# First layer's recurrence: the state-free part made for eight chunks at once, a short chain left

## The chip, the core and the metric

The kernel runs on one core of one Trainium2 chip. Its engines work from queues of their own: PE multiplies matrices into PSUM, DVE and POOL work on vectors, ACT evaluates functions and copies, SP and POOL issue the transfers. The metric is the device time of one execution in microseconds, lower is better; between runs it varies by some tenths of a per cent.

## What is computed

Two layers of a streaming encoder, 2048 tokens of width 1024, all in float32. The change is in the first layer: a state of 64x64 for each of 12 heads, updated token by token.

```python
def step(state, inp):
    r_t, w_t, k_t, v_t, kk_t, a_t = inp
    sa = jnp.einsum('bhvk,bhk->bhv', state, -kk_t)
    state = (state * w_t[:, :, None, :]
             + sa[..., None] * (kk_t * a_t)[:, :, None, :]
             + v_t[..., None] * k_t[:, :, None, :])
    y_t = jnp.einsum('bhvk,bhk->bhv', state, r_t)
    return state, y_t
...
for l in range(DEPTH):
    h = rms_norm(x, pre_norm[l])
    # l = 0: proj = h @ a_w_in, y_br = rwkv7_time_mix(z, ...)
    # l = 1: y_br = diff_attention(q, k_sh, v_sh, ...)
    y_mem = memory_cross_attention(q_mem, mem_n, w_mem_kv[l])
    y = concatenate([y_br * silu(gate), y_mem * silu(g_mem)]) @ w_out[l]
    x = x + rms_norm(y, post_norm[l])
```

`kk_t` is the key times a gain, normalised to length one in each head (`rsqrt` of the sum of its squares); `a_t` is a sigmoid and `w_t` the decay, both from small projections.

## The kernel before

The first layer works in 24 steps: 2 halves of the sequence, in each 6 pairs of heads, in each 2 blocks of 512 tokens. A block has 8 chunks of 64 tokens. Within a chunk the recurrence is solved as a triangular system of 64x64, so that only the state passes from chunk to chunk. A step is an object with these parts (line numbers are those of the kernel before):

- `p1`: the projections of key, receptance and value for 512 tokens (`pj`, L174: 24 products of 128x512 each, hi and lo parts of weights and input in turn), the small products `lr` (L323, L324), decay and sigmoid (`cum`, `asg`), the key's normalisation `pss`/`rn` (L341 to L348), and the operands `AR` and `BK` of the chunk products.
- `p2`: products `pg` of all chunks (L380), masked to `Gm` on DVE (L383); transposes `BKT` (L391) and `UV`.
- `p3`: the triangular inverse `TT`. On DVE a chain of 15 dependent pairs of small operations (`itmp` L431, `Ti` L433), set into two transposed copies (`T16` L440, `TT16` L444); then on PE the products `inv` (L455, twice), `invz` (L468) and `invr` (L474).
- `p4`: the chain over 8 chunks. Each: `xy` (L493, L496), a copy `xs` on ACT, `us` (L502), a copy `UV` on DVE (L503), `sps` (L507), the new state `sb` on DVE (L510), with the decayed state `SP` made on POOL (L491), and the output `xy` (L513).
- `p5`: the norm of the output over each head, a transpose `py` (L535), gate, store.

The loop at the end of `layer_a` traces `p4(i)`, `p5(i)`, `p2(i+1)`, `p3(i+1)` and then `filler(i+2)`: the gate projection of step i+1 (again 24 `pj`) and `p1` of step i+2. From that the framework's scheduler makes, when the program is built, a fixed order for each engine; each engine then works through its order and waits at its head. PSUM tiles come from rings: `pj`, `lr`, `pbn` share three banks under the tag `pj`; most others use two under `gm`, the chain three of its own.

Of the kernel before, what the change touches and what calls it, by code (L numbers as in the profile page):

```python
# [59 lines left out]
def hybrid_kernel(ctx, tc, S, HALF, x, mem, pv, cv, dist, postn, w_out, w_mkv, a_w, w2, a2, w_kv, b_w, out):  # L60
# [68 lines left out]
    def rstd_(xt, junk, ss):  # L129
        """junk: where the squares go; ss: a column for each part of the rows"""  # L130
# [5 lines left out]
    def rows_T(xt, ps, dst, eng):  # L136
        """512 columns of 128 rows, transposed, to each hi, lo of dst, with its gain; eng rounds to hi"""
# [13 lines left out]
    def norm_T(rows, dst, pool, W, PS, xt=None, ptag="gm", eng=nc.sync, junk=None):  # L151
        """128 rows of DRAM (or xt), normalised and transposed into each hi, lo of dst, with its gain"""
# [26 lines left out]
    def mem_T(h, m0, W, PS, pool):  # L179
        """the memory, normalised for both layers, transposed"""  # L180
# [4 lines left out]
    def mem_kv(h, tile_, W, load, PS):  # L185
        """for both layers, keys (hi over lo) and values of the memory, to DRAM"""
# [22 lines left out]
    def layer_a(ph):  # L209
# [46 lines left out]
        def PS(shape, name, tag="gm", bufs=2):  # L256
# [49 lines left out]
        class Step:  # L306
            """one head pair, one block of TB tokens"""
# [4 lines left out]
            def p1(self):  # L312
# [23 lines left out]
                kk2 = W([P, TB], "kk2")  # L336
                A.activation(kk2, kk, AF.Square)
                pss = PS([P, NJ, 2], "pss")
                for c in range(NC):
                    rows = slice(64, 128) if c % 2 == 0 else slice(0, 64)  # L340
                    mm(pss[rows, c // 2, :], lhsT=kk2[:, c * C:(c + 1) * C], rhs=bsum, start=True, stop=True)  # L341
                rn = T([P, NC, 2], "rn", 3)
# [307 lines left out]
        for i in range(n):  # L650
# [626 lines left out]
```

## Time and profile before

| | |
|---|---|
| runs of the program, median (lowest to highest of 3) | 3232.57 us (3231.21 to 3237.78) |
| span of the profiled execution, first to last instruction | 3242.7 us, 10.1 us (0.3%) above that median |
| busy share: PE, DVE, ACT, POOL | 95%, 62%, 44%, 29% |
| mean granted TensorE clock | 0.977 |
| chain that ended last | PE 76%, DVE 14%, ACT 4% |

The span is what the trace counts; no other time is given for the profiled execution itself. Busy shares are means over the whole span; the 24 steps take the stretch from about 70 to 1560 us, the second layer the rest. A busy PE is not a PE at its peak, since starts of matmuls overlap; where a price matters, it is read from the time between starts.

### The profile page before, as it was taken

The page shows a single profiled execution, that of the slowest core. Times are in us where ns is not written, and L with a number is a line of the kernel's source. Part 1 is how long each engine was busy: PE and PEld are TensorE (multiplying, and loading weights), DVE is VectorE, ACT ScalarE, POOL GpSimd, SP SyncE. Part 2 cuts the span into 40 slices and gives each one's busy share as a digit, 9 for nine tenths or more (in the row PEclk, how much of TensorE's full clock was granted, in tenths as well). Part 3 has the DMA queues.
Part 4 walks back from the last instruction along what each step waited for, and adds up shares of the span by engine and source line. Part 5 has one row for each costly group of instructions (what it writes and reads, how often), then busy time and mean ns, then how long its engine had stood idle before and what let it go on. Part 6 is the DMA issues. An engine that isn't in the chain of part 4 may idle for free.

```text
span 3242.7 us, 53751 instructions
## 1 busy us (share of the span) xinstructions
PE 3074.5 (95%) x20026; PEld 2404.1 (74%) x20026; DVE 2008.1 (62%) x5546; ACT 1421.3 (44%) x3126; POOL 928.4 (29%) x1092
## 2 busy tenths in 40 slices
PE   6899999998899999999899999999999999999999
PEld 4766767676667676767577798898887878877777
DVE  6678777866687878786456411111106888887554
ACT  6524333434443434333345522222315777777443
POOL 3224434443244334433100121312411332222100
PEclk9989999998899999999899999999999999999999
DMA  4201000113210001002554443423436555444453
GB/s 131 75 16 35 27 22 22 34 40 90 57 35 27 23 22 33 29 18 69 136 147 135 134 113 90 117 74 96 117 110 159 118 116 112 102 85 119 118 154 113
DMA packets 266150, 265.21 MB, mean 82 GB/s; under 512 B 16832, under 2 KB 206656, under 8 KB 265760
## 3 DMA queue, kind: packets, MB, share of 16 engines
q1 hardware_dynamic: 237760, 195.31, 20.7%
q0 software_dynamic: 28128, 66.46, 10.1%
q8 instruction: 157, 2.57, 0.3%
q14 instruction: 105, 0.86, 0.1%
HBM read 180.45 MB, written 81.26 MB: 81 GB/s over the span
## 4 chain that ended last, share of the span: by engine, by line
PE 76%; DVE 14%; ACT 4%; issue 3%; DMA 2%; POOL 1%; SPq 0%; DVEq 0%; ACTq 0%; POOLq 0%
PE pj L174 30%; PE po L820 10%; PE o L1135 5%; PE vps L996 4%; PE pg L380 3%; PE s L1094 3%; PE s L1095 2%; PE us L502 2%; PE xy L496 2%; PE tr L1125 2%; PE sps L507 1%; PE xy L493 1%; PE mo L759 1%; PE xy L513 1%; DVE E L1097 1%
## 5 line engine op out<-in xcount | busy, mean ns | idle before, releaser
L174 PE MATMUL pj<-hhi,wh 128*128 128x512 f32 x928 | 395.3, 426 | 2.2 <-DVE hlo L149 1.7
L174 PE MATMUL pj<-hhi,wl 128*128 128x512 f32 x928 | 393.2, 424 | 0.4 <-POOL wl L123 0.4
L174 PE MATMUL pj<-hlo,wh 128*128 128x512 f32 x928 | 385.0, 415 | 0.0
L123 POOL TENSOR_TENSOR wl<-wraw,wh 128x512 fp32r<-128x512 f32 x168 | 221.0, 1327 | 399.8 <-ACT wh L122 372.2
L1097 DVE CUSTOM_DVE_ANT_0 E<-s,dist 128x512 f32<-128x512 f32 (+1 forms) x480 | 276.2, 605 | 35.0 <-PE s L1095 28.9
L174 PE MATMUL pj<-bh,wh 128*128 128x512 f32 x672 | 262.6, 391 | 0.0
L174 PE MATMUL pj<-bl,wh 128*128 128x512 f32 x672 | 262.4, 391 | 0.0
L174 PE MATMUL pj<-bh,wl 128*128 128x512 f32 x672 | 262.3, 390 | 0.0
L1102 ACT ACTIVATE E<-E,nm 128x1920 f32<-128x1920 f32 (+7 forms) x192 | 229.4, 1199 | 59.1 <-DVE nm L1100 58.6
L491 POOL TENSOR_SCALAR SP<-sb,PC 128x128 f32<-128x128 f32 x192 | 119.5, 624 | 469.7 <-DVE sb L510 469.7
L1135 PE MATMUL o<-th,vs 128*128 128x256 f32 (+1 forms) x864 | 211.0, 376 | 2.3 <-ACT th L1128 0.9
L174 PEld LDWEIGHTS pj<-hhi,wh 128*128 128x128 f32 x928 | 178.5, 192 | 45.6 <-ACT hhi L148 3.3
L1094 PE MATMUL s<-ks,qd 128*128 128x512 f32 (+1 forms) x480 | 205.7, 432 | 2.2 <-DVE mx L1097 1.2
L174 PEld LDWEIGHTS pj<-hhi,wl 128*128 128x128 f32 x928 | 177.6, 191 | 38.9 <-POOL wl L123 0.8
L174 PEld LDWEIGHTS pj<-hlo,wh 128*128 128x128 f32 x928 | 178.2, 192 | 33.9 <-issue 0.2
L122 ACT ACTIVATE wh<-wraw 128x512 fp32r<-128x512 f32 x168 | 105.4, 628 | 198.0 <-PE pj L174 138.9
L1135 PEld LDWEIGHTS o<-th,vs 128*128 128x128 f32 x864 | 153.8, 189 | 38.7 <-ACT th L1128 19.4
L514 ACT ACTIVATE ys<-xy 64x128 f32<-64x128 f32 x192 | 52.0, 271 | 297.0 <-PE xy L513 251.5
L1095 PE MATMUL s<-ks,qd 128*128 128x512 f32 (+1 forms) x480 | 176.2, 373 | 0.0
L510 DVE SCALAR_TENSOR_TENSOR sb<-sps,PC,SP 64x64 f32<-64x64 f32 x384 | 108.4, 282 | 64.9 <-PE sps L507 57.0
L174 PEld LDWEIGHTS pj<-bh,wh 128*128 128x128 f32 x672 | 126.6, 188 | 26.4 <-DVE ot L831 0.3
L174 PEld LDWEIGHTS pj<-bl,wh 128*128 128x128 f32 x672 | 126.6, 188 | 26.2
(401 smaller groups left out, 7342.3 us busy)
## 6 DMA issues: line engine op xcount, KB each, us to landing
wraw<-in_a_w SPq DMA_DIRECT2D x126, 256.0 KB, 2.9
qd<-qd_d POOLq DMA_DIRECT2D x48, 512.0 KB, 6.9
mq<-mq POOLq DMA_DIRECT2D x64, 256.0 KB, 4.3
ks<-ks_d POOLq DMA_DIRECT2D x24, 512.0 KB, 6.5
yr<-y_dram SPq DMA_DIRECT2D x31, 384.0 KB, 4.9
xt<-in_x SPq DMA_DIRECT2D x16, 512.0 KB, 5.3
x_dram<-ot SPq DMA_DIRECT2D x16, 512.0 KB, 4.4
wraw<-in_b_w SPq DMA_DIRECT2D x32, 256.0 KB, 3.0
```

What stands on the lines that cost most here:

```text
L122: A.activation(hi[:, ks], raw, AF.Copy)
L123: eng.tensor_tensor(out=lo[:, ks], in0=raw, in1=hi[:, ks].bitcast(F32), op=ALU.subtract)
L174: mm(ps, lhsT=w[a_][:, k, wcol], rhs=h[b_][:, k, tsl], start=n == 0, stop=n == 3 * KT - 1)
L491: G_.tensor_scalar(out=SP, in0=SB, scalar1=PC[:, c:c + 1], scalar2=None, op0=ALU.mult)
L510: V.scalar_tensor_tensor(out=SB[hc, hc], in0=sp[hc, :], scalar=PC[hc, c:c + 1], in1=SP[hc, hc], op0=ALU.mult, op1=ALU.add)
L820: mm(po[hf], lhsT=a_[:, k, :], rhs=b_[hf][:, k, :], start=k == i == 0, stop=k == KT - 1 and i == 2)
L996: mm(ps[:, t, :], lhsT=hT[b][a_][:, k, tsl], rhs=w[b_][:, k, :], start=n == 0, stop=n == 3 * KT - 1)
L1094: mm(ps[:, f:f + w_], lhsT=qd[:, 0, c, qs], rhs=k_[:, c, 0:w_], start=True, stop=False)
L1095: mm(ps[:, f:f + w_], lhsT=qd[:, 1, c, qs], rhs=k_[:, c, 0:w_], start=False, stop=True)
L1097: V.tensor_tensor_reduce(out=e[:, kb * 512:kb * 512 + w], in0=ps[:, 0:w], in1=dt_[:, u0:u0 + w], scale=-SLOPES[h], scalar=3.0e38, op0=ALU. ...
L1102: A.activation(E[c][:, 0:nk], E[c][:, 0:nk], AF.Exp, bias=nm[:, c:c + 1], scale=-1.0, accum_out=nm[:, 2 + c:3 + c])
L1135: mm(po[:, oc], lhsT=vs[kt // 4][:, kt % 4, :], rhs=th[:, rc], start=n == 0, stop=n >= nmm - 2, skip_group_check=True)
```

## The change

`p4` is split. The new `p4` (traced after `p3`, one step ahead) makes for all eight chunks at once what needs no state: transposes `atp`, products `nvp`, both solved with `TT` in `txp`, then for each chunk a 128x128 matrix `MT` (identity plus a product, `mrp`) and a 128x64 matrix `RT`, and it starts the sums `ch` with the chunk's own input. `p4b` is the chain: for each chunk one product with `MT` (128x128 by 128x64) onto `ch`, and one scaled copy on ACT, which is the next state; the outputs `yp` are products with `Gm` and with `RT`. The state is kept as 128x64. The key's normalisation is put into `kk` itself: `pss` is now one product of 128x512 with the block of ones, in the ring `pj`, and its inverse comes from Ln and Exp on ACT and a product on POOL; so `Gm` is a masked copy of 512 columns at once (4 operations instead of 32) and `BKT` a plain copy, now on ACT. `pg` takes the two heads in turn. The second `lr` product uses all 128 rows. The rings: `gm` has three banks, the chain two. Comments went, and two constants of the second layer (`ones`, `epsd`) moved to a pool opened later.

```diff
-pps = str_.enter_context(pool_(name="pps", bufs=2, space=PSUM, side="right"))
+pps = str_.enter_context(pool_(name="pps", bufs=3, space=PSUM, side="right"))
...
-def PS(shape, name, tag="gm", bufs=2):
+def PS(shape, name, tag="gm", bufs=3):
...
-            mm(pl, lhsT=lora[rows, 2], rhs=th[i][rows], start=False, stop=True)
+            mm(pl, lhsT=lora[:, 2 + i], rhs=th[i], start=False, stop=True)
...
-        kk2 = W([P, TB], "kk2")
...
-     
+        rn = W([P, TB], "rn")
+        A.activation(rn, kk, AF.Square)
+        pss = PS([P, TB], "pss", "pj")
+        mm(pss, lhsT=bones, rhs=rn, start=True, stop=True)
+        V.tensor_scalar(out=rn, in0=pss, scalar1=1e-12, scalar2=None, op0=ALU.max)
+        A.activation(rn, rn, AF.Ln)
+        A.activation(rn, rn, AF.Exp, scale=-1.0)
+        G_.tensor_tensor(out=rn, in0=rn, in1=asg, op=ALU.mult)
...
-        G_.tensor_tensor(out=kk, in0=kk, in1=asg, op=ALU.mult)
+        G_.tensor_tensor(out=kk, in0=kk, in1=rn, op=ALU.mult)
...
-        for g in range(2):
+        for e in range(2):
+            pgs = [PS([P, NJ, P], "pg") for hh in range(2)]
+            for j in range(NJ):
+                for hh in range(2):
+                    hs = slice(hh * 64, hh * 64 + 64)
+                    mm(pgs[hh][:, j, :], lhsT=BK[hs, 2 * j + e, :], rhs=AR[hs, 2 * j + e, :], start=True, stop=True)
             for hh in range(2):
-                pg = PS([P, 4, P], "pg")
...
-        BKT = T([P, NC, P], "BKT", 2)
+                V.tensor_tensor(out=Gm[:, e, :, hh, :], in0=pgs[hh], in1=cc(("maskE", "maskO")[e], 128)[:, None, :].broadcast_to([P, NJ, P]), op=ALU.mult)
+        BKT = T([P, NC, P], "BKT", 1)
         for g in range(2):
             pt = PS([P, 4, 2, 64], "bkp")
             for c in range(4):
                 nc.tensor.transpose(pt[:, c].rearrange("p h k -> p (h k)"), BK[:, g * 4 + c, :], ident)
-            V.tensor_tensor(out=BKT[:, g * 4:g * 4 + 4, :].rearrange("p c (h k) -> p (c h) k", h=2),
-                            in0=pt.rearrange("p c h k -> p (c h) k"),
-                            in1=rn[:, g * 4:g * 4 + 4, :].rearrange("p c h -> p (c h)")[:, :, None].broadcast_to([P, 8, 64]), op=ALU.mult)
+            A.activation(BKT[:, g * 4:g * 4 + 4, :], pt.rearrange("p c h k -> p c (h k)"), AF.Copy)
...
-        AR, Gm, BKT, UV, PC = self.AR, self.Gm, self.BKT, self.UV, self.PC
-        ys = self.ys = T([P, NJ, 2, 64], "ys", 1)
-        SB = sb[self.p]
+        AR, Gm, BKT, UV, TT = self.AR, self.Gm, self.BKT, self.UV, self.TT
+        ar = (slice(64, 128), slice(0, 64))
+        rr = (slice(0, 64), slice(64, 128))
+        hcs = (slice(0, 64), slice(64, 128))
+        X = [I([P, 2, 2, P], "X") for g in range(2)]
+        pt = PS([P, NJ, P], "atp")
+        for j in range(NJ):
+            for e in range(2):
+                mm(pt[ar[e], j, :], lhsT=AR[:, 2 * j + e, ar[e]], rhs=ident, start=True, stop=True)
+        for g in range(2):
+            A.activation(X[g][:, :, :, 0:C], pt.rearrange("p j (h k) -> p j h k", h=2)[:, g * 2:g * 2 + 2], AF.Copy, scale=-1.0)
+        pn = PS([P, NJ, 2, C], "nvp")
+        for j in range(NJ):
+            for hh in range(2):
+                for e in range(2):
+                    c = 2 * j + e
+                    mm(pn[ar[e], j, hh, :], lhsT=Gm[rr[e], e, j, hh, ar[e]], rhs=UV[rr[e], c, hcs[hh]], start=True, stop=True)
+        for g in range(2):
+            A.activation(X[g][:, :, :, C:P], pn[:, g * 2:g * 2 + 2], AF.Copy, scale=-1.0)
+        Wn = I([P, NJ, 2, C], "Wn")
+        UV4 = UV.rearrange("p (j e) (h v) -> p j e h v", e=2, h=2)
+        for g in range(2):
+            js = slice(g * 2, g * 2 + 2)
+            px = PS([P, 2, 2, P], "txp")
+            for j in (g * 2, g * 2 + 1):
+                for hh in range(2):
+                    for e in range(2):
+                        mm(px[ar[e], j % 2, hh, :], lhsT=TT[ar[e], j, hh, :], rhs=X[g][ar[e], j % 2, hh, :], start=True, stop=True)
+            A.activation(Wn[:, js], px[:, :, :, 0:C], AF.Copy)
+            for e in range(2):
+                A.activation(UV4[ar[e], js, e], px[ar[e], :, :, C:P], AF.Copy)
+        MT = T([P, NC, P], "MT", 1)
+        MT4 = MT.rearrange("p (j e) k -> p j e k", e=2)
+        RT = T([P, NC, C], "RT", 1)
+        for hh in range(2):
+            G_.memset(MT[hcs[hh], :, hcs[1 - hh]], 0.0)
+        AR4 = AR.rearrange("p (j e) t -> p j e t", e=2)
+        pmr = [PS([P, NJ, P], "mrp") for e in range(2)]
+        for j in range(NJ):
+            for hh in range(2):
+                for e in range(2):
+                    mm(pmr[e][hcs[hh], j, 0:C], lhsT=Wn[ar[e], j, hh, :], rhs=BKT[ar[e], 2 * j + e, hcs[hh]], start=True, stop=True)
+                    mm(pmr[e][hcs[hh], j, C:P], lhsT=Wn[ar[e], j, hh, :], rhs=Gm[ar[e], e, j, hh, rr[e]], start=True, stop=True)
+        for e in range(2):
+            for hh in range(2):
+                hs = hcs[hh]
+                V.tensor_tensor(out=MT4[hs, :, e, hs], in0=pmr[e][hs, :, 0:C], in1=ident[hs, None, hs].broadcast_to([C, NJ, C]), op=ALU.add)
+            V.tensor_tensor(out=RT.rearrange("p (j e) t -> p j e t", e=2)[:, :, e], in0=pmr[e][:, :, C:P], in1=AR4[:, :, e, rr[e]], op=ALU.add)
+        ch = pps.tile([P, NC, C], F32, name="ch", tag="ch", bufs=2)
         for c in range(NC):
-            j, e = c // 2, c % 2
...
-            mm(xy, lhsT=AR[:, c, :], rhs=SB, start=True, stop=True, skip_group_check=True)
             for hh in range(2):
-                hc = slice(hh * 64, hh * 64 + 64)
...
-            A.activation(ys[rr, j].rearrange("p h v -> p (h v)"), xy[rr], AF.Copy)
+                mm(ch[hcs[hh], c, :], lhsT=BKT[:, c, hcs[hh]], rhs=UV[:, c, hcs[hh]], start=c == 0, stop=False, skip_group_check=True)
+        self.MT, self.RT, self.ch = MT, RT, ch
+    def p4b(self):
+        Gm, UV, PC, ch, MT, RT = self.Gm, self.UV, self.PC, self.ch, self.MT, self.RT
+        hcs = (slice(0, 64), slice(64, 128))
+        b = self.t0 // TB
+        S = T([P, NC, C], "S", 1)
+        st = [sb[self.p][:, b % 2]] + [S[:, c] for c in range(1, NC)] + [sb[self.p][:, 1 - b % 2]]
+        for c in range(NC):
+            mm(ch[:, c, :], lhsT=MT[:, c, :], rhs=st[c], start=False, stop=True, skip_group_check=True)
+            A.activation(st[c + 1], ch[:, c, :], AF.Copy, scale=PC[:, c:c + 1])
+        ys = self.ys = T([P, NJ, 2, C], "ys", 1)
+        py = [PS([P, NJ, C], "yp") for hh in range(2)]
+        for hh in range(2):
+            for j in range(NJ):
+                for e in range(2):
+                    rr = hcs[e]
+                    mm(py[hh][rr, j, :], lhsT=Gm[:, e, j, hh, rr], rhs=UV[:, 2 * j + e, hcs[hh]], start=j == 0, stop=False, skip_group_check=True)
+        for j in range(NJ):
+            for e in range(2):
+                for hh in range(2):
+                    c, rr = 2 * j + e, hcs[e]
+                    mm(py[hh][rr, j, :], lhsT=RT[hcs[hh], c, :], rhs=st[c][hcs[hh]], start=False, stop=True, skip_group_check=True)
+        for hh in range(2):
+            A.activation(ys[:, :, hh], py[hh], AF.Copy)
...
-    steps[i].p4()
+    steps[i].p4b()
...
         steps[i + 1].p2()
         steps[i + 1].p3()
+        steps[i + 1].p4()
```

The order of PE changes around the small products. Before, in a regular step (`lr` of the step after next, then the receptance's `pj`, then `inv` of the next step; numbers behind names are tile numbers):

```order
L323 MATMUL lr<-th_9224,lora 128x512
L324 MATMUL lr<-th_9224,lora 128x512
L323 MATMUL lr<-th_9227,lora 128x512
L324 MATMUL lr<-th_9227,lora 128x512
L174 MATMUL pj<-hhi,wh 128x512
L174 MATMUL pj<-hlo,wh 128x512
L174 MATMUL pj<-hhi,wl 128x512
L174 MATMUL pj<-hhi,wh 128x512
L174 MATMUL pj<-hlo,wh 128x512
L174 MATMUL pj<-hhi,wl 128x512
L455 MATMUL inv<-T_10352,E_10292 64x64 x9
```

After the change, at the same place in another regular step:

```order
L174 MATMUL pj<-hlo,wh 128x512
L174 MATMUL pj<-hhi,wl 128x512
L319 MATMUL lr<-th_8434,lora 128x512
L320 MATMUL lr<-th_8434,lora 128x512
L319 MATMUL lr<-th_8437,lora 128x512
L320 MATMUL lr<-th_8437,lora 128x512
L335 MATMUL pss<-rn,cvt 128x512
L442 MATMUL inv<-T_10741,E_10681 64x64 x16
L174 MATMUL pj<-hhi,wh 128x512
L174 MATMUL pj<-hlo,wh 128x512
L174 MATMUL pj<-hhi,wl 128x512
```

The first of the receptance's `pj` has moved behind `pss` and `inv`; ahead of `pss` stand the last of the key's 24 `pj` (22 of them stand between `pg` with its transposes and `lr`) and the four `lr`. Steps of this kind, called A below, are 8 (steps 3, 5, 7, 9, 15, 17, 19, 21). In 11 others, called B, `inv` stands first, then `pss`, then the second `inv`, with nothing between. In A the copy of the first `inv` stands on ACT behind the Ln and Exp of `rn`, and on DVE `TT` behind both `BK`; in B they stand ahead. In steps 1, 11, 12 and 23 there are 41 to 51 `pj` ahead of `inv`.

On PE, the chain before, one chunk and the start of its neighbour's end:

```order
L493 MATMUL xy<-sb_124,AR 128x128
L496 MATMUL xy<-UV,Gm 64x64 x2
L174 MATMUL pj<-hhi,wh 128x512
L174 MATMUL pj<-hlo,wh 128x512
L502 MATMUL us<-xs,TT 64x64 x2
L174 MATMUL pj<-hhi,wl 128x512
L174 MATMUL pj<-hhi,wh 128x512
L174 MATMUL pj<-hlo,wh 128x512
L507 MATMUL sps<-UV,BKT 64x64 x2
L513 MATMUL xy<-UV,Gm 64x64 x2
```

And after, three chunks of the new chain:

```order
L174 MATMUL pj<-hhi,wh 128x512
L174 MATMUL pj<-hlo,wh 128x512
L537 MATMUL ch<-S,MT 128x64
L551 MATMUL yp<-S,RT 64x64 x2
L174 MATMUL pj<-hhi,wl 128x512
L537 MATMUL ch<-S,MT 128x64
L551 MATMUL yp<-S,RT 64x64 x2
L174 MATMUL pj<-hhi,wh 128x512
L174 MATMUL pj<-hlo,wh 128x512
L537 MATMUL ch<-S,MT 128x64
L551 MATMUL yp<-S,RT 64x64 x2
```

Between two links of the chain there are now one or two `pj` instead of some eight; the other `pj` stand in a block ahead of the chain (28 in A, 36 in B) and one behind it (19).

On DVE, what stands ahead of `kk`, which ACT squares for `pss`. Before:

```order
L442 TENSOR_SCALAR X_10348<-Ti,cvt 128x16x16 x2
L280 SCALAR_TENSOR_TENSOR kx<-pj,pvt,kx 128x511
L444 STREAM_TRANSPOSE TT_10356<-X_10348 128x16x32
L538 TENSOR_TENSOR ys<-ys,bon 128x512
L281 SCALAR_TENSOR_TENSOR kx<-carry,pvt,kx 128x1
L326 TENSOR_SCALAR cum<-cum 128x8x64
L282 COPY carry<-pj 128x1
L326 TENSOR_SCALAR asg<-asg 128x512
L458 TENSOR_TENSOR TT<-inv,TT_10356 128x512
L461 STREAM_TRANSPOSE Ta<-TT 128x256
L330 SCALAR_TENSOR_TENSOR cum<-cvt,cum 128x520
L335 TENSOR_SCALAR kk<-kx,pvt 128x512
```

After, in the step of kind A whose PE rows stand above:

```order
L418 TENSOR_TENSOR itmp<-Dd,Ti 128x15
L326 SCALAR_TENSOR_TENSOR cum<-cvt,cum 128x520
L420 TENSOR_TENSOR Ti<-Ti,itmp 128x15
L331 TENSOR_SCALAR kk<-kx,pvt 128x512
L425 TENSOR_SCALAR X_10738<-Ti,cvt 128x16x16 x2
L345 TENSOR_TENSOR AR<-kk,Pt 128x4x128
L427 STREAM_TRANSPOSE T_10741<-X_10738 128x16x32
L429 TENSOR_SCALAR X_10737<-Ti,cvt 128x16x16 x2
L353 COPY PC<-Pt 128x8
L431 STREAM_TRANSPOSE TT_10745<-X_10737 128x16x32
```

In both, `kk` (from the step after next) stands behind the `Ti` chain and behind the scan `cum`; what has moved is what PE holds ahead of `pss`. Ahead of the rows shown there stand in the new order, from the four `Gm` on: two transposes of 64x512, one `e_sil`, two `Dd`, the `Ti` chain, and in it `kx` and the minima of `cum` and `asg`. In B the scan, the transposed copy `T` and `kk` come in this order.

## Rows read from the trace of the kernel before

**Rows 1.** The page's head: span, busy time of PE, granted clock by slice

```profile
span 3242.7 us, 53751 instructions
...
PE 3074.5 (95%) x20026; PEld 2404.1 (74%) x20026; DVE 2008.1 (62%) x5546; ACT 1421.3 (44%) x3126; POOL 928.4 (29%) x1092
...
PEclk9989999998899999999899999999999999999999
```

**Rows 2.** Busy time of a regular stretch: PE, PEld, DVE, ACT, POOL, clock, DMA

```profile
980.00:1460.00 480.00, 460.65 (x3792) 333.62 (x3791) 384.77 (x1117) 175.49 (x386) 189.31 (x225) 0.99 0.09 26
```

**Rows 3.** Line L535 from 900 to 1500 us: ns min/median/max, first and last start

```profile
L535 PE MATMUL py<-cvt,ys x40: 272/273/329, 961.1 to 1456.6; 128*128 128x128 f32 x40
```

**Rows 4.** PE in order of time, one chunk of the chain: start, length in us

```profile
1213.77 0.38 PE L493 MATMUL xy<-sb,AR 128*128 128x128 f32 x2
1214.08 0.44 PE L496 MATMUL xy<-UV,Gm 64*64 64x64 f32 x4
1214.45 0.50 PE L174 MATMUL pj<-hhi,wl 128*128 128x512 f32 x1
1214.79 0.40 PE L174 MATMUL pj<-hhi,wh 128*128 128x512 f32 x1
1215.11 0.44 PE L502 MATMUL us<-xs,TT 64*64 64x64 f32 x4
1215.48 0.50 PE L174 MATMUL pj<-hlo,wh 128*128 128x512 f32 x1
1215.82 0.39 PE L174 MATMUL pj<-hhi,wl 128*128 128x512 f32 x1
...
1216.52 0.39 PE L174 MATMUL pj<-hhi,wl 128*128 128x512 f32 x1
1216.83 0.34 PE L507 MATMUL sps<-UV,BKT 128*64 128x64 f32 x4
1217.00 0.40 PE L513 MATMUL xy<-UV,Gm 128*64 128x64 f32 x4
1217.33 0.50 PE L174 MATMUL pj<-hhi,wh 128*128 128x512 f32 x1
```

**Rows 5.** PE in order of time: other small products and what follows them

```profile
1173.21 0.50 PE L323 MATMUL lr<-th,lora 128*128 128x512 f32 x1
1173.64 0.49 PE L324 MATMUL lr<-th,lora 64*128 64x512 f32 x1
...
1179.59 1.15 PE L455 MATMUL inv<-T,E 64*64 64x64 f32 x32
1180.66 0.50 PE L174 MATMUL pj<-hhi,wh 128*128 128x512 f32 x1
...
1204.28 1.16 PE L380 MATMUL pg<-AR,BK 64*128 64x128 f32 x8
1205.37 0.50 PE L174 MATMUL pj<-hlo,wh 128*128 128x512 f32 x1
```

**Rows 6.** DVE by line and form, 980 to 1460 us: count, busy us, mean ns

```profile
L330 DVE TENSOR_TENSOR_SCAN cum<-cvt,cum 128x520 f32<-128x520 f32 x8 | 14.2, 1775 | 0.8 <-ACT cum L328 0.8
...
L438 DVE TENSOR_SCALAR X<-Ti,cvt 128x256 f32<-128x256 f32 x18 | 12.3, 682 | 0.0
L391 DVE TENSOR_TENSOR BKT<-bkp,rn 128x512 f32<-128x512 f32 x18 | 12.0, 686 | 0.2
...
L440 DVE STREAM_TRANSPOSE T<-X 128x512 f32<-128x512 f32 x9 | 9.4, 1042 | 0.0
...
L280 DVE SCALAR_TENSOR_TENSOR kx<-pj,pvt,kx 128x511 f32<-128x511 f32 x9 | 6.7, 750 | 0.3
```

**Rows 7.** DVE in order of time, inside the `Ti` chain

```profile
1217.90 0.18 DVE L431 TENSOR_TENSOR itmp<-Dd,Ti 128x15 f32<-128x15 f32 x1
...
1219.56 0.21 DVE L433 TENSOR_TENSOR Ti<-Ti,itmp 128x48 f32<-128x48 f32 x1
```

**Rows 8.** ACT by line and form, 980 to 1460 us

```profile
L498 ACT ACTIVATE xs<-xy 64x128 f32<-64x128 f32 x71 | 19.3, 272 | 70.4 <-PE xy L496 69.3
...
L337 ACT ACTIVATE kk<-kk 128x512 f32<-128x512 f32 x8 | 4.9, 614 | 0.0
```

**Rows 9.** Stretches around two drops of the granted clock, columns as in rows 2

```profile
1188.00:1192.00 4.00, 4.00 (x51) 3.20 (x52) 3.39 (x9) 0.26 (x1) 1.27 (x1) 0.50 0.00 0
...
1570.00:1574.00 4.00, 0.00 (x0) 0.00 (x0) 4.00 (x4) 2.23 (x5) 3.49 (x4) 0.51 0.42 117
...
1578.00:1582.00 4.00, 0.21 (x1) 0.21 (x2) 1.61 (x3) 1.99 (x3) 1.62 (x3) 0.50 1.10 386
```

More of the change, by code (lines that the diff above doesn't have):

```diff
@@ L230, in layer_a @@
         for p in range(NPAIR):
-            t = pa.tile([P, P], F32, name=f"sb{p}")
-            G_.memset(t, 0.0)
+            t = pa.tile([P, 2, C], F32, name=f"sb{p}")
+            G_.memset(t[:, 0], 0.0)
             sb.append(t)
@@ L335, in p1 @@
                 V.tensor_scalar(out=kk, in0=kx, scalar1=pc("k_k", p), scalar2=None, op0=ALU.mult)
-                kk2 = W([P, TB], "kk2")
[L337 to L342, printed above, removed]
-                G_.memset(rn, 1.0)
-                rt = TL([P, NJ, 2], "rt", 2)
-                V.tensor_scalar(out=rt, in0=pss, scalar1=1e-12, scalar2=None, op0=ALU.max)
-                rn4 = rn.rearrange("p (j e) h -> p j e h", e=2)
-                V.reciprocal(out=rn4[64:128, :, 0, :], in_=rt[64:128])
-                V.reciprocal(out=rn4[0:64, :, 1, :], in_=rt[0:64])
+                rn = W([P, TB], "rn")
[6 more added lines that the diff above has]
+                G_.tensor_tensor(out=rn, in0=rn, in1=asg, op=ALU.mult)
                 AR = T([P, NC, P], "AR", 2)
@@ L573, in load_lora @@
                     nc.sync.dma_start(out=raw[r:r + 64, i], in_=src[:, p * P:(p + 1) * P])
-            l = pw.tile([P, 3, P], F32R, name="lora", tag="lora", bufs=1)
+            l = pw.tile([P, 4, P], F32R, name="lora", tag="lora", bufs=1)
             A.activation(l[:, 0:2], raw, AF.Copy)
-            for i in range(2):
-                rows = slice(i * 64, i * 64 + 64)
-                G_.tensor_tensor(out=l[rows, 2], in0=raw[rows, i], in1=l[rows, i].bitcast(F32), op=ALU.subtract)
+            G_.tensor_tensor(out=l[:, 2:4], in0=raw, in1=l[:, 0:2].bitcast(F32), op=ALU.subtract)
             return l
@@ L640, in load_mem @@
             return w_
-        mem_kv(memT, lambda sh, n_, dt: T(sh, n_, 2, "BKT", dt=dt), lambda sh, n_: T(sh, n_, 2, "sil"), load_mem, PS)
+        mem_kv(memT, lambda sh, n_, dt: T(sh, n_, 4, "iv", dt=dt), lambda sh, n_: T(sh, n_, 2, "sil"), load_mem, PS)
+        steps[0].p4()
         filler(1)
@@ L1174, in hybrid_kernel @@
     op = layer_a(ph.enter_context(pool_(name="ph", bufs=NB)))
+    const2 = ctx.enter_context(pool_(name="const2", bufs=1, side="right"))
+    ones = const2.tile([P, P], F32, name="ones")
+    epsd = const2.tile([P, P], F32, name="epsd")
     layer_b_proj(ph, op)
```

47 lines of the change are left out of this document (5 added, 42 removed).

## The prediction

> **What bounds the kernel now.** I read the page's head first: PE is busy 95% of the span [rows 1]. Since the change is in the first layer alone, I then asked for a regular stretch of its steps, 980 to 1460 us: PE busy 460.65 of 480 us, 96%, at a clock of 0.99; DVE 80%, ACT 37%, POOL 39% [rows 2]. So here PE's own work sets the time, and the chain's round trips are hidden: PE's order holds `pj` products between every two of its links [rows 4]. How long a step takes I read from the ten transposes `py` of that stretch: 961.1 to 1456.6 us is nine steps, 55.06 us each [rows 3]. Of that PE idles 4%, 2.2 us. The question is therefore not how short the chain gets, but what the change does to PE's work and to PE's waits.
>
> **What is removed.** I price small products by the time from their start to the next group's start, since their lengths overlap. One chunk [rows 4]: `xy` 0.31 (1213.77 to 1214.08), its second part 0.37, `us` 0.37, `sps` 0.17, the output 0.33; together 1.55. A `pj` inside a block takes 0.233 ((1216.52 - 1215.82) / 3), but 0.34 right behind such a group and 0.31 or 0.32 right ahead of one; that is some 0.1 at five such places, 0.49. So a chunk costs PE 2.04 us, a step of eight 16.3 us. The trace shows a loss of time at each change between the small products and the full array. The Trainium skill, "TensorEngine Tiling (Array Packing)", Key Properties, has the reason: changing the tiling mode drains the engine. By the 0.1 of rows 4, the new kernel's nine or so changes a step cost 2 us.
>
> **What is added on PE**, a step, in records (each float32 product is two). The trace has the prices: 0.033 for 64x64 products that go round the quarters of the array (1.07 us for 32, 1179.59 to 1180.66 [rows 5]), 0.043 where the two column halves alternate (`sps`, 0.17 for 4), 0.083 to 0.093 in one quarter, 0.136 (`pg`, 1.09 for 8 [rows 5]) to 0.155 (`xy`) for 128 columns. `atp` 16 x 0.07 = 1.1 (bounds 0.7 and 2.2); `nvp` 32 x 0.033 = 1.1 (to 3.0); `txp`, 128 columns but two halves at a time, 32 x 0.06 = 1.9 (1.1 to 4.4); `mrp`, four records in a quarter and then the next, 64 x 0.052 = 3.3 (2.1 to 6.0); `ch` 32 x 0.043 = 1.4 (to 2.7); the chain 16 x 0.08 = 1.3 (0.7 to 2.5); `yp` from `Gm` 32 x 0.043 = 1.4 (to 2.7) and from `RT` 32 x 0.04 = 1.3 (1.1 to 3.0); changes of tiling 2.0 (1.4 to 3.0). Sum 14.8, bounds 11 and 29; I take 14.8, because nearly all of these are issued in the alternating order that `inv` and `sps` have. `pg` goes from 32 x 0.136 = 4.4 to 3.3, since half of it alternates heads now. PE's work falls by 16.3 - 14.8 + 1.1 = 2.6 us a step. `pss` as one product, `lr` on all rows: nothing, between 0 and -0.7.
>
> **What moves, and what waits.** The order of PE is fixed, and that is where I expect the loss. After `pg` PE holds the transposes, 22 `pj`, four `lr`, and then `pss` or `inv`; the receptance's `pj`, which need neither, come behind. Counted from the start of `py`, PE has until then: `py` 0.6, `pg` 3.3, twelve transposes about 1.6, 22 x 0.233 = 5.1, `lr` 4 x 0.43 = 1.7 [rows 5]: 12.3 us. `pss` needs `kk` from DVE and its square from ACT. DVE can start `Gm` some 2.4 us after `py` starts (transposes, ACT's and DVE's 512 columns, about 0.7 each). Then, in its order: four `Gm` at 0.69 (the nearest row, another 128x512 from PSUM [rows 6]), 2.7; two transposes of 1.04, 2.1; `Dd` and `e_sil`, 1.3 (half and full width, estimates below the 0.69); 30 operations of the `Ti` chain at 0.237 ((1219.56 - 1217.90) / 7 [rows 7]), 7.1; `kx` 0.75 and its two columns, 1.1; the two minima, 0.9; the scan 1.78 [rows 6]; `kk` 0.5. That is 17.5; queued operations overlap a little (-1), and the `Ti` chain must wait for POOL's clearing of `Ti`, which stands behind POOL's work on `Gm` (+1 to +2): 18. With ACT's copy ahead and its square, 0.61 [rows 8], and the hand-overs, `pss` can start 2.4 + 18 + 1.4 = 21.8 us after `py`. PE stands still for 21.8 - 12.3 = 9.5 us; I take 10 (bounds 5 and 13). In B `inv` comes first and needs one more transpose (1.04): the same 10. Before, the chain's own products and their `pj` filled that time: `p4` of the step before lay between `pg` and `inv`.
>
> Behind it: in A, the first `inv` is copied by ACT only after Ln and Exp of `rn`, 0.6 each, and `TT` stands on DVE behind two products that POOL feeds: PE waits 0.4 + 1.4 + 2.0. In B 0.6. In both, `py` comes 0.5 us before its norm is ready, since only 19 `pj` (4.4 us) cover it.
>
> The chain: a link needs PE's product, a copy (0.27 on 64x128 [rows 8]) and two hand-overs, about 0.7; PE has 0.75 to 1.0 of work per link. It costs nothing further; without the `pj` it would be 0.
>
> DVE loses the state's and `UV`'s operations, 28 of 32 `Gm`, and gains six adds; POOL loses `SP`. ACT gains some 5 us a step and stays under half. None of these bounds the whole step; DVE bounds the stretch above because its operations there hang on each other.
>
> **The clock.** After a stretch without products the granted clock is at half: 0.51 and 0.50 with PE idle at 1570 to 1582 us, and 0.50 for 1188 to 1192 us, with PE busy all the time, behind its smallest products [rows 9]. Ten idle microseconds in each step should bring this each time; part of the slow work lies in waits. I take 1.5 us a step (0 to 3.5). The Trainium skill, "TensorE: Matmul & The Clock Gate", HAM oscillation, warns of exactly such idle gaps between blocks of products. By that rule each of the 19 stalls would end at half clock and the cost be nearer the 3.5, some 38 us more in all.
>
> **The sum.** A step of kind A: -2.2 (the old idle time, counted anew) - 2.6 + 10 + 3.8 + 0.5 = +9.5; of kind B: -4.8 + 10 + 0.6 + 0.5 = +6.3. Eight A: 76; eleven B: 69; the other five have 41 to 51 `pj` there or a start of their own, about +1 each, 5; the clock 19 x 1.5 = 28. Together +178 on the profile's 3242.7, 3421; the span lies 10 above the median of the runs, so on the median 3232.6 + 178 = **3410 us**. The first 70 us and the second layer stay.
>
> **Rivals.** (1) *Faster*: DVE's stretch hides and PE stays the bound. Then -2.6 x 24 = -62, and with half of the idle time gone -26 more: 3145 to 3170. It decides at DVE's 18 us: below 9 nothing waits. For it: DVE has lost much work. Against: what was lost lies elsewhere; every operation of the stretch has a row or a near one. 9%. (2) The chain's link is longer than thought, 1.1 to 1.4 us instead of PE's 0.9, so that PE waits at each: 0.4 x 8 x 24 = +77, 3487. Before, `us` started 1.03 us after `xy`'s second part [rows 4], with two `pj` between. The change would then not do what it says, make the chain short. 10%. (3) The small products cost nearer the upper bounds, say 19: +100, 3510. 14%. (4) The losses just cancel: stalls of 3 us a step, no change. 3%. My forecast: 64%.
>
> **Numbers.** Faster 0.09, same (within 0.2%, about what runs of this kernel can tell) 0.03, slower 0.88. The forecast's own range is 3330 to 3480: stalls of 7 to 12 us, clock 0 to 3.5. With rivals (2) and part of (3), and stalls of 5 us below, 3280 to 3520 holds 8 in 10.
>
> **What would show it.** PE busy in a regular stretch down to 80 to 85%; waits of some 10 us at `inv` or `pss`, released by DVE's `T` or ACT's `rn`; a step of 61 to 65 us; half clock once a step behind the wait; DVE busy without a break from `Gm` to `kk`. I am wrong if PE stays above 95% and a step is near 50 us, or if the long waits are at `ch`.

## The result, and the profile after

The changed kernel takes 3376.18 us (3373.14 to 3379.96, three runs): 1.0442 times the kernel before, with a 95% interval of 1.0423 to 1.0461, so 143.6 us slower. The forecast was 178 us slower, and the time lies in the range.

The page's head of the kernel after, beside [rows 1]:

```profile
span 3374.4 us, 57447 instructions
...
PE 3006.6 (89%) x22378; PEld 2437.8 (72%) x22378; DVE 1816.6 (54%) x4728; ACT 1515.2 (45%) x3318; POOL 866.6 (26%) x936
...
PEclk8898998988888898998999999999999999999899
```

The span grew by 131.7 us while PE's busy time fell by 68 us, and DVE lost 191.5 us of work; ACT gained 94 us and stays at 45%. No engine got more to do that could explain the time. The clock's row loses tenths in the first half, where the first layer is. The regular stretch of the first layer (columns as in [rows 2]) and the whole layer from its first `py` to its last, in the kernel after:

```profile
980.00:1460.00 480.00, 396.56 (x4104) 315.75 (x4098) 281.64 (x724) 194.55 (x418) 158.39 (x156) 0.90 0.08 25
179.00:1702.00 1523.00, 1253.93 (x12750) 1000.54 (x12749) 873.99 (x2247) 620.85 (x1356) 472.33 (x463) 0.90 0.12 34
```

The whole layer before, cut the same way:

```profile
193.50:1567.40 1373.90, 1302.97 (x10399) 953.00 (x10399) 1045.49 (x2998) 524.87 (x1163) 522.60 (x601) 0.97 0.13 37
```

PE is busy 83% of the regular stretch, where it was 96% [rows 2], and the clock is 0.90 instead of 0.99. The transposes at a step's start, beside [rows 3]:

```profile
L574 PE MATMUL py<-cvt,ys x40: 270/272/273, 1015.1 to 1567.9; 128*128 128x128 f32 x40
```

Nine steps in 552.8 us, 61.4 us a step against 55.06. What PE waited for in the first layer (engine and line that waited, what it waited for: us in total, times, longest):

```profile
PE inv L442 <- POOL wl L123: 77.5, 8, 9.7
PE pss L335 <- ACT rn L333: 74.3, 11, 8.6
PE inv L442 <- DVE T L427: 49.6, 7, 10.4
PE invz L455 <- DVE Ta L448: 18.1, 8, 2.9
...
PE ch L537 <- ACT S L538: 9.5, 10, 2.3
```

Before, the largest wait at `inv` or `pss` was

```profile
PE inv L455 <- DVE T L440: 13.4, 11, 2.9
```

The waits at `inv` and `pss` are now 201.4 us; those at the chain's products `ch` are 9.5. One wait of the first row, PE in order of time:

```profile
1085.57 0.39 PE L319 MATMUL lr<-th,lora 128*128 128x512 f32 x1
1085.79 0.39 PE L320 MATMUL lr<-th,lora 128*128 128x512 f32 x1
1095.87 1.97 PE L442 MATMUL inv<-T,E 64*64 64x64 f32 x32 [9.69 <-POOL wl L123]
1097.77 2.07 PE L335 MATMUL pss<-rn,cvt 128*128 128x512 f32 x2
```

and DVE at the same time:

```profile
1093.55 1.22 DVE L326 TENSOR_TENSOR_SCAN cum<-cvt,cum 128x520 f32<-128x520 f32 x1
1094.69 1.03 DVE L427 STREAM_TRANSPOSE T<-X 128x512 f32<-128x512 f32 x1
```

The profile names POOL's `wl`, but `T` ends at 1095.72 and `inv` starts 0.15 us later. It does so in all fifteen waits at `inv`, whichever engine is named, so all are waits for DVE's `T`. And `inv` takes 1.9 us where it took 1.07 in [rows 5]: the granted clock is 0.51 from 1088 to 1102 us, half clock (1.2 GHz, the lower of the two levels), in the wait and behind it.

To see the three parts of the loss I took the layer from the first `py` to the last, 23 steps, for each kernel: PE's busy time and the rest (idle) as in the row above, and the trace's clock records laid over PE's busy time, which gives how much of it ran at half clock. Half of that is time lost to the clock; busy time less this loss is PE's work at full clock. All in us a step:

| kernel | step | idle | lost to the clock | work |
|---|---|---|---|---|
| before | 59.74 | 3.08 | 1.42 | 55.2 |
| after | 66.22 | 11.70 | 3.97 | 50.5 |

(The mean holds some long steps, so it is above the regular step.) Over 23 steps that is +198 us of idle time, +59 us lost to the clock and -108 us of work: +149 us. PE's work did fall, and more than forecast; idle time and clock together took back more than twice of it.

### The profile page after: what moved, and what is told of

It is laid out like the page before. It is cut to its first block, busy times and chain, and to the rows that moved or that the text cites. A ratio compares the mean times of both kernels' runs of the same rounds, so it can differ in the third digit from the quotient of the medians.

```text
span 3374.4 us, 57447 instructions
## 1 busy us (share of the span) xinstructions
PE 3006.6 (89%) x22378; PEld 2437.8 (72%) x22378; DVE 1816.6 (54%) x4728; ACT 1515.2 (45%) x3318; POOL 866.6 (26%) x936
## 5 line engine op out<-in xcount | busy, mean ns | idle before, releaser
L174 PE MATMUL pj<-hhi,wl 128*128 128x512 f32 x928 | 377.0, 406 | 0.7 <-POOL wl L123 0.7
L174 PE MATMUL pj<-hlo,wh 128*128 128x512 f32 x928 | 375.9, 405 | 0.0
L442 PE MATMUL inv<-T,E 64*64 64x64 f32 x768 | 45.4, 305 | 127.1 <-POOL wl L123 77.5
L442 PEld LDWEIGHTS inv<-T,E 64*64 64x64 f32 x768 | 41.5, 213 | 145.1 <-issue 84.6
L174 PEld LDWEIGHTS pj<-bh,wl 128*128 128x128 f32 x672 | 126.6, 188 | 26.2
```

Of the source, the lines that this page charges most:

```text
L174: mm(ps, lhsT=w[a_][:, k, wcol], rhs=h[b_][:, k, tsl], start=n == 0, stop=n == 3 * KT - 1)
L442: mm(pb[rows, j, hh, :], lhsT=lt[rows, j, hh, :], rhs=rt_[rows, j, hh, :], start=True, stop=True)
```

## Experiments

My theory at the start: PE idles because its fixed order runs out of work before DVE's stretch from `Gm` to `T` and `kk` ends; the old chain used to lie there and covered it, that is, gave PE work while DVE was busy. Rivals: the added small products cost it; the chain's links are too slow. Each ratio is to the kernel before, run on the same chip between (its median was 3235.37 to 3236.46 us).

**DVE's stretch cut short** (the kernel then leaves out 14 of the 15 rounds of the `Ti` chain, so it does not compute the inverse and stands for the time alone):

```diff
-                for j in range(15):
+                for j in range(1):
```

> Leaves out 14 of the 15 iterations of the 16x16 triangular inverse on DVE, 28 small instructions of about 0.24 us, 6.6 us of DVE's stretch between Gm and T in each step; PE's work is the same. The order of PE changes with it (the products of the norm come behind inv). Theory (PE waits for that stretch): the wait of 7 to 10 us a step falls by 6 to 7 us, the half clock behind it mostly goes too: 54 to 56 us a step, 3190 to 3250 us. Rival (more small products on PE, or the links of the chain): DVE has half its time free already, so 3360 to 3380 us.

Measured: 3211.91 us, 0.8 per cent faster than before (0.9917, 0.989 to 0.9943), 164 us below after. PE's instructions are the same 22378; their order shifts a little, with `pss` behind `inv`. So DVE's stretch bounds the changed kernel: the cut is worth 6.8 us a step, and the small products and the links are not what makes it slow.

**The order, in two edits.** One puts `pss` into the ring of the small products, so that the receptance's `pj` need not wait behind it:

```diff
-                pss = PS([P, TB], "pss", "pj")
+                pss = PS([P, TB], "pss")
```

The other writes the next step's state-free part ahead of this step's chain:

```diff
         for i in range(n):
+            if i + 1 < n:
+                steps[i + 1].p2()
+                steps[i + 1].p3()
             steps[i].p4b()
...
             if i + 1 < n:
-                steps[i + 1].p2()
-                steps[i + 1].p3()
                 steps[i + 1].p4()
```

> The product of the key norms (pss) gets its place from the ring of the small products instead of the ring of the projections; nothing else is edited. TensorE's order then has 13 to 19 more projection products ahead of the triangular products (inv), and pss behind the chunk starts (ch). Theory (PE idles behind pss and inv because its fixed order runs out of work before DVE's stretch from Gm to T ends): 15 products of 0.23 us, 3.5 us, more cover in the steps that had pss first, none of the wait in front of inv gone otherwise; the wait falls from 7 to 10 us a step to 4 to 7, and the time by 2 to 4 us in each of 24 steps: 3280 to 3330 us. Rival 1 (the added small products are what costs): nothing is removed, 3365 to 3385 us. Rival 2 (the chain's links): the chain loses 16 products of cover, so 3376 us or more.

> The state-free part of the next step (the pair products pg with Gm, Ti and T) is written ahead of the chain of this step, so that the eight links and about 37 projection products lie between pg and inv; the same instructions otherwise. Theory (the cover of DVE's 18 to 19 us stretch was lost): PE has 3.9 us of bkp and pvt, about 8 us of chain and 8.5 us of projections there, some 20 us, so the wait of 7 to 10 us in front of inv or pss and the half clock behind it go: a step falls from 61.4 us to 50 to 53 us, below the 55.06 us of before, and the time to 3110 to 3190 us. Rival 1 (the added small products cost more than the old chain): they are all still there, so no less than 3340 us. Rival 2 (the latency of a link, product to ScalarE and back, bounds): the links now have 2 products between them instead of 3 or 4, so 3376 us or more.

> Both edits: the state-free part of the next step ahead of this step's chain, and pss in the ring of the small products. Theory: with the chain as cover, pss no longer waits for long where it stands, so the second edit is worth 0 to 2 us a step on top: 3080 to 3190 us. Rival (pss in the ring of the projections is the whole loss, the chain's place none): the same time as with the edit of pss alone. Rival (the added small products): no less than 3340 us.

Measured: `pss` alone 3387.42 us (1.0468, 1.0432 to 1.0505), 11 us worse than after, a miss; the chain's place alone 3274.93 us (1.011, 1.0081 to 1.0139), 101 us better, but well above what I expected; both 3212.89 us (0.992, 0.9898 to 0.9942), 0.8 per cent faster than before and also above the expected range. So neither is the whole cause: the first is worth nothing alone and 62 us on top of the second. Why, the waits show. With the chain early alone, PE's waits at `inv` and `pss` fall from 201.4 to 53.2 us, but it now stands in front of `py`, for the norm of the output on DVE:

```profile
PE py L574 <- DVE ys L571: 91.5, 18, 7.0
PE pss L335 <- ACT rn L333: 27.0, 7, 6.0
PE inv L442 <- DVE T L427: 26.2, 18, 4.1
```

With `pss` moved alone:

```profile
PE inv L442 <- DVE T L427: 68.0, 18, 7.7
PE pbn L391 <- POOL kx L357: 50.8, 19, 4.0
PE inv L442 <- POOL wl L123: 19.3, 4, 5.0
```

and with both:

```profile
PE pg L371 <- DVE BK L351: 68.4, 22, 3.9
...
PE inv L442 <- DVE T L427: 11.3, 10, 2.6
```

Once the first wait is gone, PE waits for the keys: at `pbn` for POOL's `kx` (there the key times the receptance), or at `pg` for `BK`. That pointed away from the chain, to the normalisation.

**The parts of the change alone.** The chain with the old normalisation; the normalisation with the old chain; and the changed kernel with lora's low part read on 64 rows again:

```diff
-                    mm(pl, lhsT=lora[:, 2 + i], rhs=th[i], start=False, stop=True)
+                    rows = slice(i * 64, i * 64 + 64)
+                    mm(pl, lhsT=lora[rows, 2], rhs=th[i][rows], start=False, stop=True)
```

The other two are the parts of the diff shown ahead, put together the other way: the lines from `rn` to `BKT` from the one kernel, `p4` and `p4b` (or `p4`) from the other. The full rows of lora and the new sizes of the rings go with the chain.

> The chain part of the change alone: the state-free products, the one 128x128 product and scaled copy per chunk, and lora's full rows, with the normalisation of before (16 small products for the norms in the ring of the small products, 16 masked and scaled DVE instructions for Gm, the scaled BKT on DVE). Theory (the loss is the lost cover of DVE's stretch between pg and T by the chain): the loss stays here, 3330 to 3420 us; DVE's stretch is longer by the 16 instructions for Gm, but 48 projection products lie ahead of inv. Rival (the new normalisation, its product pss with its late rn, makes the loss): near before, 3210 to 3260 us.

> The normalisation part of the change alone on the kernel before: the norm as one 128x512 product in the ring of the projections, the keys scaled ahead of pg, four instructions for Gm, BKT a plain ScalarE copy; the old chain of the recurrence stays and lies between pg and inv. Theory: the old chain covers DVE's stretch as before, and pss stands inside the chain, where its wait is shared with the chain's own: 3190 to 3270 us, within 1 per cent or so of before. Rival (the normalisation makes the loss): 3320 us or more.

> Undoes the full rows of lora's low part alone in the kernel after: lr's second product reads 64 rows again, as before, where lr's four products took 0.43 us each against 0.23 us after. Theory (PE waits for DVE behind them in half of the steps, where the time is swallowed): 0 to 12 us slower than after, 3376 to 3390 us. Rival (PE's work bounds in each step): 0.8 us in each of 24 steps, 19 us or more, 3395 us.

Measured: the chain alone 3268.08 us (1.0102, 1.0081 to 1.0123), the normalisation alone 3311.04 us (1.0234, 1.0212 to 1.0257). Both miss, and the wrong way round: the normalisation costs 76 us by itself, the chain 33, and together they cost some 35 more than the sum. My theory had all of it in the chain. In the chain alone PE stands mostly at `pbn`, for a POOL product that comes behind DVE's operations, and less at `inv`:

```profile
PE pbn L401 <- POOL kx L364: 85.1, 18, 10.1
PE inv L452 <- DVE T L437: 29.3, 15, 6.5
```

The 64 rows of lora: 3373.84 us, the same as after, as expected. PE's work rises by 0.6 us a step and its idle time falls by 0.6 (the table below): `lr` stands ahead of the wait, which takes in what it saves.

**The chain early, with the old normalisation** (the chain alone, with the edit of the order in the loop):

> The chain part alone, with the normalisation of before, and the state-free part of the next step (pg, Gm, Ti, T) written ahead of the chain. Theory: chain and projections cover DVE's stretch, and the keys need no late rn in front of pg, which PE waits for 3 us a step where both edits of the earlier runs were made together (3212.89 us): 68 us of waits go, and DVE's longer Gm, some 4 us a step, gives a part of it back at inv: 3150 to 3230 us. Rival (links of the chain): not below 3240 us.

Measured: 3207.84 us (0.9917, 0.9897 to 0.9938). The place of the chain is worth 60 us here, and the new chain in this place is 0.8 per cent faster than the old one.

**What the normalisation costs.** Two rivals: `pss` in the ring of the projections, or the keys that come later because `BK` now needs the norm, by way of POOL. In the run with the normalisation alone PE's waits lie along the old chain, and there is none for `BK`; the longest of them:

```profile
PE sps L498 <- DVE UV L494: 22.4, 30, 1.6
PE xy L484 <- DVE sb L501: 18.4, 27, 1.6
...
PE inv L446 <- DVE T L431: 16.3, 12, 5.1
```

First `pss` moved, in the kernel with the normalisation alone (the edit as above):

> The normalisation part alone on the kernel before, as in the run that gave 3311.04 us, but with pss in the ring of the small products. Theory (pss in the ring of the projections holds back the 48 projection products of the receptance, so that invz, invr and the first chunk of the old chain run bare, with waits of 1 to 2 us and the half clock behind them): 13 to 19 of these products move ahead of pss, and the time goes back to 3215 to 3255 us. Rival (the norm's later keys in front of pg make the loss, wherever pss stands): 3290 us or more.

Measured: 3315.42 us (1.0254, 1.0206 to 1.0303), no gain. My theory fell, and the rival named what to look for. The time is the same, but the waits have moved; the longest is now

```profile
PE pg L375 <- DVE BK L355: 62.5, 21, 4.7
```

So I moved the three multiplications of the key path off POOL:

```diff
-                G_.tensor_tensor(out=rn, in0=rn, in1=asg, op=ALU.mult)
+                V.tensor_tensor(out=rn, in0=rn, in1=asg, op=ALU.mult)
...
-                G_.tensor_tensor(out=kk, in0=kk, in1=rn, op=ALU.mult)
+                V.tensor_tensor(out=kk, in0=kk, in1=rn, op=ALU.mult)
...
-                G_.tensor_tensor(out=kx, in0=kx, in1=asg, op=ALU.mult)
+                V.tensor_tensor(out=kx, in0=kx, in1=asg, op=ALU.mult)
```

> The normalisation part alone on the kernel before, with pss in the ring of the small products (3315.42 us), and the three multiplications of the key path on DVE in place of POOL. In that run PE waited 62.5 us in front of pg for DVE's BK, 3 us in each of 21 steps. Theory (the late keys in front of pg make the loss of the normalisation part, by this wait and the half clock behind it): 3 us a step go at least, 3225 to 3260 us. Rival (the wait passes on to the chain of small DVE and PE instructions of the recurrence, which DVE's added 2 us a step delays, or other work of the new norm costs it): 3290 us or more.

Measured: 3241.5 us (1.0014, 0.9989 to 1.0039), no longer slower than before, and 74 us below the run with `pss` moved (whose four runs spread from 3299.61 to 3333.51). The wait fell to less than half:

```profile
PE pg L375 <- DVE BK L355: 28.2, 20, 3.6
```

**The same three multiplications on DVE in the changed kernel**, with `pss` moved; once with the chain behind `inv` as in the change, once ahead:

> The kernel after with pss in the ring of the small products, and three 128x512 multiplications of the key path (rn by the rate, kk by rn, kx by the rate) on DVE, where such a one takes 0.69 us, in place of POOL, where it takes 1.28 us and stands behind the weights' low parts. The chain stays behind inv. With pss moved alone the time was 3387.42 us, with 51 us of waits for POOL's kx and 87 us for DVE's T. Theory (lost cover of DVE's stretch and late keys both count): the 51 us and a part of the half clock go, those for T stay: 3290 to 3345 us. Rival (the late keys are the whole loss): 3260 us or less. Rival (the place of the chain is the whole loss): 3370 us or more.

> The version with pss in the ring of the small products and the next step's state-free part ahead of the chain (3212.89 us), with the same three multiplications on DVE in place of POOL. In that version PE waited 68.4 us in front of pg for DVE's BK, 3 us in each of 22 steps, and POOL had these three and two low parts of weights in a row before it. Theory: BK comes 3 to 5 us earlier, the wait in front of pg goes, and DVE, idle there, takes on 2 us a step: 1 to 3 us a step, 3140 to 3190 us. Rival (the wait passes on to inv or py, behind DVE): 3200 to 3220 us.

Measured: 3319.28 us (1.0252, 1.0227 to 1.0278) and 3150.98 us (0.9746, 0.9732 to 0.9761). The three multiplications are worth 68 and 62 us here. With keys in time the place of the chain decides over 168 us. The second is the fastest version of all, 2.5 per cent faster than before. The key path shows why. In the version with both order edits, POOL, and the last operation of the path on DVE:

```profile
1125.66 1.29 POOL L123 TENSOR_TENSOR wl<-wraw,wh 128x512 fp32r<-128x512 f32 x1 [6.11 <-ACT wh L122]
1127.27 1.74 POOL L123 TENSOR_TENSOR wl<-wraw,wh 128x512 fp32r<-128x512 f32 x1 [0.31 <-ACT wh L122]
1128.97 1.29 POOL L339 TENSOR_TENSOR rn<-rn,asg 128x512 f32<-128x512 f32 x1
1130.34 1.28 POOL L346 TENSOR_TENSOR kk<-kk,rn 128x512 f32<-128x512 f32 x1
1131.98 1.64 POOL L350 TENSOR_TENSOR kx<-kx,asg 128x512 f32<-128x512 f32 x1 [0.36 <-DVE asg L349]
1133.65 0.69 DVE L351 TENSOR_TENSOR BK<-kx,cum 128x512 f32<-128x512 f32 x1 [1.16 <-POOL kx L350]
```

and in the fastest, DVE:

```profile
1132.01 0.68 DVE L339 TENSOR_TENSOR rn<-rn,asg 128x512 f32<-128x512 f32 x1
1132.73 0.69 DVE L346 TENSOR_TENSOR kk<-kk,rn 128x512 f32<-128x512 f32 x1
1133.34 0.54 DVE L349 TENSOR_SCALAR asg<-asg,pvt,oka 128x512 f32<-128x512 f32 x1
1133.80 0.68 DVE L347 TENSOR_TENSOR BK<-kk,cum 128x512 f32<-128x512 f32 x1
1134.40 0.68 DVE L350 TENSOR_TENSOR kx<-kx,asg 128x512 f32<-128x512 f32 x1
1135.12 0.69 DVE L351 TENSOR_TENSOR BK<-kx,cum 128x512 f32<-128x512 f32 x1
```

On POOL the three take 1128.97 to 1133.62, behind two low parts of weights, and the path up to the end of `BK` 5.4 us; on DVE it takes 3.8. How much of the gain is POOL's longer operations, how much its queue, and how much DVE's `asg`, which is slower beside POOL (last section), no run separates. The waits of the fastest:

```profile
PE inv L442 <- DVE T L427: 46.7, 23, 4.6
PE py L574 <- DVE ys L571: 20.0, 21, 1.7
PE pg L371 <- DVE BK L351: 19.6, 21, 3.2
```

The balance of all, worked out as above:

| kernel | median us | step | idle | lost to the clock | work |
|---|---|---|---|---|---|
| `Ti` chain cut | 3211.91 | 59.24 | 6.1 | 2.1 | 51.0 |
| lora on 64 rows | 3373.84 | 65.99 | 11.1 | 3.7 | 51.1 |
| `pss` moved | 3387.42 | 66.67 | 9.1 | 7.3 | 50.2 |
| chain early | 3274.93 | 59.95 | 8.2 | 3.1 | 48.6 |
| both | 3212.89 | 57.88 | 6.0 | 4.0 | 47.9 |
| `pss` moved, keys on DVE | 3319.28 | 64.18 | 8.1 | 5.6 | 50.4 |
| both, keys on DVE | 3150.98 | 54.97 | 5.3 | 1.2 | 48.5 |
| chain alone | 3268.08 | 61.55 | 7.6 | 2.9 | 51.2 |
| chain alone, early | 3207.84 | 57.37 | 6.8 | 2.6 | 48.0 |
| normalisation alone | 3311.04 | 62.45 | 5.1 | 3.6 | 53.8 |
| the same, `pss` moved | 3315.42 | 62.16 | 4.9 | 3.7 | 53.5 |
| the same, keys on DVE | 3241.50 | 59.69 | 3.2 | 2.7 | 53.8 |

(With the chain early the first `py` comes 30 to 36 us later, so its 23 steps lack a part of the first step's work; compare the last column inside that group. The second layer's edges move the medians a little too.) The work of the new chain's versions lies 4 to 5 us a step under that of before (and, for the reason given, 6.6 to 7.3 with the chain early) whatever the time; idle time and clock decide.

## Why the prediction was right, and where it was off

*What bounds it.* Right: PE's work was the bound before, and the change was decided by PE's waits. The links (rival 2) don't count: 9.5 us of waits at `ch` in the whole layer.

*Removed and added products.* The sign was right, the size off. PE's work fell by 4.7 us a step as a mean of the 23, and by 5.5 in the 19 steps of kinds A and B, not by 2.6. A regular step's new products in the kernel after, by their starts:

```profile
1229.36 1.09 PE L481 MATMUL atp<-cvt,AR 128*64 128x128 f32 x16
1230.38 1.15 PE L489 MATMUL nvp<-UV,Gm 64*64 64x64 f32 x32
1231.46 0.50 PE L174 MATMUL pj<-hhi,wh 128*128 128x512 f32 x1
...
1232.85 1.82 PE L500 MATMUL txp<-X,TT 64*64 64x128 f32 x29 [0.42 <-DVE TT L463]
1234.41 0.27 PE L515 MATMUL mrp<-BKT,Wn 64*64 64x64 f32 x1
...
1235.20 0.37 PE L515 MATMUL mrp<-BKT,Wn 64*64 64x64 f32 x8 [0.35 <-ACT UV L503]
...
1236.38 0.80 PE L526 MATMUL ch<-UV,BKT 128*64 128x64 f32 x20
```

`atp` 1.02 (priced 1.1), `nvp` 1.08 (1.1), `txp` some 1.7 (1.9), and `mrp` 1.97 with 0.35 of waiting in it, where I had 3.3: four records in one quarter and then the next go no slower than alternating ones do. `lr` goes at 0.22 to 0.23 a product instead of 0.43 [rows 5], 0.8 us a step, which I had between 0 and 0.7. Rival 3 is refuted: these products cost less than I said, not more.

*What waits.* Right in place and mechanism: waits of 7 to 10 us at `pss` and `inv`, the one released by ACT's square of `kk` and the other by DVE's `T`, with PE at 83% and steps of 61.4 us (forecast 80 to 85% and 61 to 65). In a step of kind A, `py` at 1134.36, `pss` starts 21.2 us behind `py`; in the next, of kind B, `inv` starts 21.8 behind it. The forecast was 21.8 for `pss` and about the same for `inv`, so DVE's stretch was priced rightly, though some of its terms were not (the scan takes 1.2 us, not 1.78). In A the wait is only 7.11 us, since PE's work ahead of it took 14.1 us where I gave it 12.3, with a wait at `pg` and half clock on the way; the step takes 64.3 us (forecast 55.06 + 9.5 and 1.5 for the clock, 66.1); in B it is 9.69 and 60.0 (62.9). That DVE's stretch makes the waits is shown by the run that cuts it.

*The clock.* Too small: 50 us in the 19 steps where 28 were forecast, 59 in all 23. In the step of kind A above the granted clock was 0.51 from 1153 to 1160 us, in the wait at `pss` and behind it, and 0.57 from 1166 to 1174, around the wait at `invz` and over the small products that follow. The warning that I weighed, of the Trainium skill, "TensorE: Matmul & The Clock Gate", HAM oscillation, came a little nearer: by it I had put the cost at some 38 us more than my term, 66 in all.

*The sum.* Like for like, in the 19 steps: work -105 us for -49, idle +172 for +195 (78 for 97 in A, 94 for 98 in B), clock +50 for +28. That is +117 where I had 174. The other four between the first `py` and the last, for which I had about +1 each, grew by 32, 26 of it idle time; the last alone went from 55.8 to 73.7 us. Together 149 in the layer, where I had 178. (The span grew by 131.7 us and the medians by 143.6.) So two terms were off by about a factor of two, with opposite signs, and the steps that I hardly priced filled a part of the gap. That all 23 steps idle 198 us more, close to my 195, is luck; that the time fell into the range is owed to the mechanism and in part to these errors cancelling.

*What the working didn't see.* I gave the normalisation no price but small waits in A (1.4 us where `TT` "stands on DVE behind two products that POOL feeds", and 2.0 behind it), and told the stall as the loss of the chain's cover alone. But the normalisation costs 76 us with the old chain in its place. With `pss` in the ring that the change gave it, PE's waits there lie along the old chain; with `pss` moved the time is the same, and PE waits at `pg` for keys that go three times through POOL, and taking these off POOL brings the time back to that of before. In the kernel after no wait for the keys shows at `pg`, and PE stands still ahead of it; it shows when that is mended. So both causes are shown, the place of the chain and the late keys: each part alone is slower, the chain is mended by its place, the normalisation by the keys on DVE (with `pss` moved), and all edits together turn +4.4% into -2.5%. Not shown is what the keys on DVE are worth with `pss` left where the change put it, nor which part of the 76 us is idle time and which clock in each place; the table gives 2.0 and 2.2 us a step.

## What to carry to other kernels

When a change takes work out of a chain on the engine that bounds the kernel, ask what that chain was covering: the same instructions written at another place made 101 us here, and 168 with the keys in time. Waits in a fixed order hide each other, so an edit that gains nothing alone (`pss` moved) may be worth 62 us once the wait ahead of it is gone; try such edits together before one is dropped. Price the path to the first product of a step through each engine, queues included: three multiplications on an engine that was idle 71% of the time cost 62 to 74 us in the three pairs of runs that differ in them alone.

## What the runs showed of the hardware

The clock behind a short wait can cost much more than the wait. In the version with `pss` moved and the keys on DVE, PE stood still for 2.44 us in front of `pbn`, and then (columns as in [rows 2]):

```profile
1067.00:1083.00 16.00, 15.22 (x55) 11.21 (x56) 4.61 (x20) 3.05 (x10) 3.58 (x5) 0.50 0.10 28
```

16 us at half clock with PE busy for 15.22 of them, with the chain's links, `yp` and 17 `pj`. Some 7.6 us are lost there, in every second step. In the fastest version the layer loses 1.2 us a step to the clock in all; there the `yp` stand apart from the links, and most links have two `pj` between them. Whether the wait or the mix of products behind it kept the clock low, no run separates.

DVE's 128x512 multiplication of `asg` by a column, in the regular stretch of the kernel after, and of the fastest (count, busy us, mean ns):

```profile
L349 DVE TENSOR_SCALAR asg<-asg,pvt,oka 128x512 f32<-128x512 f32 x8 | 12.8, 1604 | 14.2 <-POOL rn L339 14.2
```

```profile
L349 DVE TENSOR_SCALAR asg<-asg,pvt,oka 128x512 f32<-128x512 f32 x9 | 4.9, 542 | 0.0
```

It takes three times as long where POOL's multiplication of `kk` starts beside it. The Trainium skill, "SBUF — State Buffer", SBUF: two separate sides, says of the ports that DVE and GpSimd share that, for a DVE operation in a two-port mode or with two inputs in SBUF, the engine that starts first holds them for its whole instruction and the other is blocked. The 1.06 us between the two rows is near POOL's 1.28 us, so the trace agrees in the length. In the order it doesn't: by the profile's starts DVE was first in all 24 steps, by 0.04 us, and was still the one that took longer. Whether this operation runs in such a mode no row shows, and no run here has this pair alone.
